# Seven-product multiplication for six column tiles instead of four, with the Fourier groups and the rotation interleaved

## The chip, the cores and the metric

The kernel runs on one core of a Trainium2 chip. The metric is the device time of one execution in microseconds; several runs are taken and the median is given. A core has five engines with their own instruction streams: TensorE (PE, matmuls), VectorE (DVE), ScalarE (ACT), GpSimd (POOL) and SyncE (SP, which here only issues transfers). Each works through its stream in order and waits where an instruction needs something that another engine or a transfer has not finished. Matmuls write to PSUM, which has eight banks of 128 x 512 floats; VectorE and ScalarE read the sums from there.

## The reference

One encoder layer is applied to 768 tokens (a prompt of 512 and a sample of 256) of width 2048:

```
h = rmsnorm(x);  z = h @ w_in            # 2048 x 2560: 1024 Fourier | 1024 q | 256 k | 256 v
of = Re(fft2 over positions and the 128 channels of each of 8 groups), then a 128 x 128 map per group
oa = banded attention on rotated q and k (16 heads, 4 key heads), with a sink per head
x  = x + concat(rmsnorm(of), rmsnorm(oa)) @ w_out
x  = x + relu(rmsnorm(x) @ w_up)**2 @ w_down;  y = rmsnorm(x)
```

The change touches the product z = h @ w_in, the Fourier part and the rotation of q and k. Everything from the attention on is the same code.

## The kernel before

All matmuls are in float32 precision built from three: an operand is split into a rounded high part and the remaining low part (`split`: a copy on ScalarE makes high, a subtraction on VectorE makes low), and high x high, high x low and low x high are summed. w_in has ten column tiles of 256: 0 to 3 Fourier, 4 to 7 queries, 8 keys, 9 values. Work runs through these stages:

**Value columns** (to 44 us): tile 9, as x arrives.

**Seven products** (44 to 161 us): tiles 0 to 3, two pairs of tiles. The weights of a pair are a matrix of 2 x 2 blocks (column tile by half of the 2048 inputs), and so is x (half of the inputs by half of the tokens, 384 each). In place of eight block products the kernel makes seven, Winograd's way, from sums of blocks. They are named a11, s1, s2, s3, a22, s4, a12 after the weight block or sum that they use. Each name takes two pairs g and two halves e of the inner dimension, so 7 x 4 = 28 products, and each product is 24 matmuls of 128 x 128 by 128 x 384 (`product7`, L277): four blocks of the inner dimension, two row halves r of 128 columns, three terms. The loop over n = 0 to 27 makes, for product n, the weight sum three ahead (`sum7`), the high part three ahead (`high7`), the low part two ahead (`low7`), things listed for this n (`high_at`, `low_at`: the sums and splits of x, and near the end `first_split`, which makes the high and low parts of the first quarter of x again for the next stage), the product, the evacuation of the product before it (`out7`) and the load five ahead (`load7`). VectorE, ScalarE and SyncE keep this order as written. PSUM: all eight banks are held, a11, s2, s3 and a22 summing up in the same four; s1, s4 and a12 in others, so that no product waits for a bank.

**Plain pieces** (161 to 365 us): tiles 8, 6, 4, 5, 7 (`cols`), each in four pieces of 48 matmuls (L815). `piece_split(p)` splits the weights of piece p and orders the load of piece p + 2. A list `todo`, filled by `after(piece, fn)`, says after which piece (or half piece) other work is written: for each Fourier group g `fold` (scaling z, sums and differences, and two small matmuls pc of the channel table cc with the map wf), `stage1` and `stage2`, and for each of four pairs of column tiles (keys, then three of the queries) the rotation: `cross` (GpSimd: z times sin), `turned` (VectorE: z times cos, then adds) and `parts` (high and low parts, stored to DRAM). Here TensorE alone keeps the order as written; SyncE, VectorE, ScalarE and GpSimd are put in order by a planner. Group g folds at g + 0.5; the rotation of the pairs begins after piece 10, when the groups are done and their tiles are freed.

The weight tiles `raw` have two buffers, `wh` and `wl` four each, shared by the seven products and the pieces: a load waits until the low part of the weights two loads before is made, and a high part waits until TensorE has finished with the product or piece four before.

## Time and profile before

| | |
|---|---|
| median of 3 runs | 2576.92 us (2576.41 to 2577.49) |
| the profiled execution | 2576.23 us, span 2574.4 us |
| PE busy | 2562.9 us, 13461 matmuls |
| DVE, ACT, POOL busy | 1795.6, 1122.5, 244.2 us |
| seven products, 44.2 to 160.8 us | 116.6 us, PE busy 116.6 |
| plain pieces, 160.8 to 364.6 us | 203.8 us, PE busy 203.8, DVE 113.6 |

A row of a group reads: line, engine, operation, output tile <- input tiles, shapes and count, then busy time in all, mean of one in ns, then the idle time of that engine just before these instructions and what ended it. The mean of a matmul is its latency: matmuls overlap, and the step from one to the next is shorter. A row of the timeline reads: start, duration, engine, line, operation, and in brackets the idle time ahead of it with what ended it. "SPq" is SyncE's queue issuing a transfer.

### The profile page before, as it was taken

The page shows a single profiled execution, that of the slowest core. Times are in us where ns is not written, and L with a number is a line of the kernel's source. Part 1 is how long each engine was busy: PE and PEld are TensorE (multiplying, and loading weights), DVE is VectorE, ACT ScalarE, POOL GpSimd, SP SyncE. Part 2 cuts the span into 40 slices and gives each one's busy share as a digit, 9 for nine tenths or more (in the row PEclk, how much of TensorE's full clock was granted, in tenths as well). Part 3 has the DMA queues.
Part 4 walks back from the last instruction along what each step waited for, and adds up shares of the span by engine and source line. Part 5 has one row for each costly group of instructions (what it writes and reads, how often), then busy time and mean ns, then how long its engine had stood idle before and what let it go on. Part 6 is the DMA issues. An engine that isn't in the chain of part 4 may idle for free.

```text
span 2574.4 us, 34791 instructions
## 1 busy us (share of the span) xinstructions
PE 2562.9 (100%) x13461; PEld 2347.1 (91%) x13461; DVE 1795.6 (70%) x2221; ACT 1122.5 (44%) x1622; POOL 244.2 (9%) x345
## 2 busy tenths in 40 slices
PE   9999999999999999999999999999999999999998
PEld 9999998888899999999999999988888888888887
DVE  7966468786565565556777777667766766777687
ACT  7645337683233333333545544433333333333335
POOL 0102322223201001100000000100000000000000
PEclk9999999999999999999999999999999999999999
DMA  7753567455755455457666666775543662554364
GB/s 290 234 186 126 170 192 214 137 160 191 229 180 176 152 174 174 163 183 240 216 232 230 213 217 211 263 290 175 178 155 118 217 230 83 175 184 159 101 210 152
DMA packets 259383, 487.84 MB, mean 189 GB/s; under 512 B 20554, under 2 KB 146512, under 8 KB 258960
## 3 DMA queue, kind: packets, MB, share of 16 engines
q1 hardware_dynamic: 187680, 321.77, 39.2%
q10 hardware_dynamic: 58512, 112.05, 11.5%
q0 software_dynamic: 13024, 51.79, 6.2%
q8 instruction: 106, 1.74, 0.3%
q14 instruction: 61, 0.50, 0.1%
HBM read 365.99 MB, written 119.54 MB: 189 GB/s over the span
## 4 chain that ended last, share of the span: by engine, by line
PE 98%; DVE 1%; DMA 0%; issue 0%; ACT 0%; SPq 0%; DVEq 0%; POOLq 0%; POOL 0%; ACTq 0%
PE pu L1209 36%; PE pd L1644 35%; PE pm L1062 10%; PE pz L815 6%; PE p L277 5%; PE pv L436 1%; PE o L940 1%; PE s L861 1%; PE t L918 1%; PE pe L644 0%; PE pa L623 0%; PE ptx L137 0%; PE pz L644 0%; DMA xr<-in_x_t 0%; PE pc L580 0%
## 5 line engine op out<-in xcount | busy, mean ns | idle before, releaser
L1209 PE MATMUL pu<-xf,wh 128*128 128x384 f32 x3072 | 780.2, 334 | 0.0
L1209 PEld LDWEIGHTS pu<-xf,wh 128*128 128x128 f32 x3072 | 554.0, 188 | 1.5 <-ACT o L1227 1.3
L1644 PE MATMUL pd<-wl,sh 128*128 128x512 f32 x1332 | 517.7, 389 | 0.0
L1644 PE MATMUL pd<-wh,sh 128*128 128x512 f32 x1332 | 517.7, 389 | 0.0
L1644 PE MATMUL pd<-wh,sl 128*128 128x512 f32 x1332 | 517.5, 389 | 0.0
L1209 PE MATMUL pu<-xf,wl 128*128 128x384 f32 x1536 | 513.1, 334 | 0.0
L1621 ACT ACTIVATE wh<-rd 128x1024 fp32r<-128x1024 f32 x200 | 202.5, 1054 | 522.1 <-PE pd L1644 424.0
L1631 DVE TENSOR_TENSOR wl<-rd,wh 128x1024 fp32r<-128x1024 f32 x200 | 236.2, 1221 | 226.1 <-ACT wh L1621 225.4
L1189 ACT ACTIVATE wh<-ur 128x1024 fp32r<-128x1024 f32 x160 | 170.1, 1063 | 382.7 <-PE pu L1209 204.4
L1644 PEld LDWEIGHTS pd<-wh,sl 128*128 128x128 f32 x1332 | 249.9, 188 | 52.2 <-DVE sl L1632 0.3
L1644 PEld LDWEIGHTS pd<-wh,sh 128*128 128x128 f32 x1332 | 250.0, 188 | 51.7
L1644 PEld LDWEIGHTS pd<-wl,sh 128*128 128x128 f32 x1332 | 250.0, 188 | 51.7
L1209 PEld LDWEIGHTS pu<-xf,wl 128*128 128x128 f32 x1536 | 288.3, 188 | 0.0
L1195 DVE TENSOR_TENSOR wl<-ur,wh 128x1024 fp32r<-128x1024 f32 x160 | 195.5, 1222 | 76.0 <-ACT wh L1189 76.0
L1230 DVE TENSOR_TENSOR o<-pu,o 128x768 f32<-128x768 f32 x160 | 152.9, 956 | 122.5 <-PE pu L1209 115.0
L1614 DVE TENSOR_TENSOR rd<-rd 128x1024 f32<-128x1024 f32 x112 | 131.8, 1218 | 0.0
L1209 PE MATMUL pu<-xs,wh 128*128 128x384 f32 x512 | 129.9, 334 | 0.0
L1189 ACT ACTIVATE wh<-sx 128x1024 fp32r<-128x1024 f32 x64 | 67.8, 1061 | 130.3 <-PE pu L1209 104.9
L277 PE MATMUL p<-xs,wh 128*128 128x384 f32 x448 | 113.7, 334 | 0.0
L1632 DVE TENSOR_TENSOR sl<-sr,sh 128x768 fp32r<-128x768 f32 x111 | 105.6, 951 | 0.0
L1195 DVE TENSOR_TENSOR wl<-sx,wh 128x1024 fp32r<-128x1024 f32 x64 | 78.2, 1223 | 24.1 <-ACT wh L1189 23.9
L1209 PEld LDWEIGHTS pu<-xs,wh 128*128 128x128 f32 x512 | 92.4, 188 | 0.0
(292 smaller groups left out, 3849.1 us busy)
## 6 DMA issues: line engine op xcount, KB each, us to landing
rd<-in_w_down SPq DMA_DIRECT2D x176, 512.0 KB, 5.2
ur<-in_w_up SPq DMA_DIRECT2D x128, 512.0 KB, 3.9
sr<-sd SPq DMA_DIRECT2D x95, 384.0 KB, 5.4
pd<-o ACTq DMA_DIRECT2D x60, 384.0 KB, 2.3
o<-pd POOLq DMA_DIRECT2D x60, 384.0 KB, 6.3
sd<-sm ACTq DMA_DIRECT2D x60, 384.0 KB, 2.9
raw<-in_w_in SPq DMA_DIRECT2D x39, 512.0 KB, 4.1
raw<-in_w_out SPq DMA_DIRECT2D x32, 512.0 KB, 4.6
```

The source lines that it names most:

```text
L277: nc.tensor.matmul(ps7[bank, g, r][:, :HALF], l[:, i, r * P : (r + 1) * P], x[:, o, 4 * e + i, :], start=(opens and e == 0 and i == 0 and ...
L815: nc.tensor.matmul(ps[c][s][:, :HALF], w[:, i, cs], whole[j // 2][s][o][:, 4 * (j % 2) + i, :], start=first and n == 0, stop=stop and n == 2,)
L1062: nc.tensor.matmul(ps, l(k), w[:, k % 2, :], start=(k == 0 and n == 0), stop=(k == 7 and n == 2))
L1189: nc.scalar.activation(wh[:], raw[:], AF.Copy)
L1195: nc.vector.tensor_tensor(out=wl[:], in0=raw[:], in1=f32(wh[:]), op=ALU.subtract)
L1209: nc.tensor.matmul(ps[:, t, :HALF], w[:, i, t * P : (t + 1) * P], xb[:, o, i, :], start=(s == first_of[bank] and i == 0 and n == 0), stop= ...
L1230: nc.vector.tensor_tensor(out=o, in0=src, in1=o, op=ALU.add)
L1614: add = lambda x, y, op: nc.vector.tensor_tensor(out=x[:], in0=x[:], in1=y[:], op=op)
L1621: nc.scalar.activation(wh[:], t[:], AF.Copy)
L1631: nc.vector.tensor_tensor(out=wl[:], in0=t[:], in1=f32(wh[:]), op=ALU.subtract)
L1632: nc.vector.tensor_tensor(out=sl[:], in0=sr[:], in1=f32(sh[:]), op=ALU.subtract)
L1644: nc.tensor.matmul(o, l[:, q, ts], w[:, ns], start=(j == j0 and (q, t) == (0, 0)), stop=(j == j1 and (q, t) == (1, 2)),)
```

## The change

Seven products now serve three pairs of column tiles, (0, 1), (2, 3) and (6, 8), the last one a quarter of the queries and the keys: 7 x 6 = 42 products. The plain pieces keep tiles 4, 5 and 7: 12 pieces. The halves r become the outer loop of a product.

PSUM is shared differently. Six banks ("x") hold the sum that runs through a11, s2, s3 and a22, one for each pair and row half. s1, s4 and a12 have a sum of their own, and these take two banks ("t") by turns. `out7(n, r)` evacuates one row half: r = 0 right after the product, r = 1 an iteration later, ahead of the next product's r = 0. The a11 sums are stored to DRAM and read back for a12 (`back7`), to free their tiles. The x steps in `high_at` and `low_at` are spread over 42 products; `first_split` comes at 35 and 38.

In the pieces, group g folds at g - 0.5, one piece earlier than before, and is loaded half a piece ahead (before: one piece). The first two pairs to be rotated (keys and the first quarter of the queries) are there from the start; the pairs are turned at 0.5, 2.5, 4.5 and 7.5, beside the groups, and the tables cos and sin are loaded before piece 0. [...]

The diff, cut to its core:

```diff
+        cols7 = ((0, 1), (2, 3), (6, 8))
+        NS7 = 2 * len(cols7)
+        NP7 = NS7 * len(names7)
...
         def product7(n):
-            w, g, e = n // 4, n // 2 % 2, n % 2
-            bank = bank7[names7[w]]
-            opens = w == 0 or names7[w] in ("s1", "a12")
+            name, g, e = of7(n)
+            own = name in ("s1", "s4", "a12")
+            opens = own or name == "a11"
             wh, wl = w7.pop(n)
-            if e == 0 and opens:
-                for r in range(2):
-                    ps7[bank, g, r] = pp.tile([P, 512], F32, **(dict(tag="f", bufs=4) if bank == "Y" and 2 * g + r < 4 else dict(tag="ps", bufs=4)), name="p7")
-            x = xs[w % 2]
-            for i in range(4):
-                for r in range(2):
+            x = xs[n // NS7 % 2]
+            for r in range(2):
+                if e == 0 and opens:
+                    ps7[own, g, r] = pp.tile([P, 512], F32, tag="t" if own else "x", bufs=2 if own else 6, name="p7")
+                for i in range(4):
...
-        def out7(n):
-            while put7:
-                put7.pop(0)()
+        def out7(n, r):
             if n < 0 or n % 2 == 0:
                 return
+            s, g, _ = of7(n)
+            ps = ps7[s in ("s1", "s4", "a12"), g, r][:, :HALF]
+            add = lambda out, x: nc.vector.tensor_tensor(out=out[:], in0=ps, in1=x[:], op=ALU.add)
...
+            elif s == "s1":
+                z = c7[1, g, r] = tile7("z11", NS7)
+                nc.scalar.activation(z[:], ps, AF.Copy)
...
+            elif s == "s4":
+                z, put = c7.pop((0, g, r)), (0, 1)
+                add(z, z)
+            else:
+                z, put = c7.pop((2, g, r)), (0, 0)
+                add(z, z)
...
+        def back7(g):
             for r in range(2):
+                z = c7[2, g, r] = tile7("z11", NS7)
+                nc.sync.dma_start(z[:], home7(g, 0, r)[:, :HALF])
...
-        step(low_at, 22, first_block)
-        step(low_at, 20, lambda: first_load(0))
+        step(low_at, 34, first_block)
+        step(low_at, 28, lambda: first_load(0))
         for e in range(2):
-            step(low_at, 24 + 2 * e, lambda e=e: first_split(e))
+            step(low_at, 35 + 3 * e, lambda e=e: first_split(e))
...
                 product7(n)
-                out7(n - 1)
+                out7(n - 1, 1)
+                out7(n, 0)
+                stores7(1 if n % 2 else 0)
                 load7(n + 5)
...
         for g in range(FG):
-            p0 = (0.5, 1.5, 2.5, 3.5, 4.5, 5.5, 6.5, 7.5)[g]
+            p0 = g - 0.5
             if g > 0:
-                after(p0 - 1, lambda g=g: load_group(g))
+                after(p0 - 0.5, lambda g=g: load_group(g))
...
-        for pair, t, ahead in ((0, 10.5, 10), (2, 11.5, None), (3, 15, None), (1, 16.5, 12)):
+        for pair, t in ((0, 0.5), (1, 2.5), (2, 4.5), (3, 7.5)):
...
+        open_rotation()
         with tc.manual_schedule(engines={mybir.EngineType.SP}):
             piece_load(0)
             piece_load(1)
+        load_z(0)
...
-    nc = bacc.Bacc("TRN2", target_bir_lowering=False, num_devices=1)
+    nc = bacc.Bacc("TRN2", target_bir_lowering=False, num_devices=1, dynamic_dma_scratch_size=4096)
```

Three places show how the order of the engines changes. The first is VectorE near the end of the seven products, around the second `first_split` (L73). In these rows wl is a low part of weights, xf the low part of x, and z<-p the add that evacuates a sum p. Before:

```order
L262 TENSOR_TENSOR wl<-raw,wh 128x1024
L70 TENSOR_TENSOR wl<-raw,wh 128x1024
L73 SCALAR_TENSOR_TENSOR xf_1608<-d_1679,gall,xf_1607 128x384 x4
L294 TENSOR_TENSOR z_892<-p_1681,z_892 128x384
L294 TENSOR_TENSOR z_894<-p_1682,z_894 128x384
L70 TENSOR_TENSOR wl<-raw,wh 128x1024 x2
```

And now:

```order
L300 TENSOR_TENSOR z_1994<-p_2119,z_1994 128x384
L272 TENSOR_TENSOR wl<-wr,wh 128x1024
L73 SCALAR_TENSOR_TENSOR xf_2038<-d_2086,gall,xf_2037 128x384 x4
L300 TENSOR_TENSOR z_1996<-p_2132,z_1996 128x384
L272 TENSOR_TENSOR wl<-raw,wh 128x1024
L70 TENSOR_TENSOR wl<-raw,wh 128x1024
```

The add of a product's first half (p_2119) stands before the split, that of its second half (p_2132) behind it; both belong to product 37 and its banks are the ones that product 38 opens again.

The second is SyncE at the transition from the products to the pieces (L237 and L331 are `load7` and `back7`, L79 the pieces' weights, cc and wf the operands of the first pc, tab a table of positions). Before:

```order
L227 DMA raw<-in_w_in 128x1024
L79 DMA raw<-in_w_in 128x1024 x6
L564 DMA cc<-in_c_chan 128x256
L559 DMA wf<-in_w_fourier 128x128
L561 DMA zf<-zf_70 128x768
L570 DMA tab<-in_c_pos 128x512
L559 DMA wf<-in_w_fourier 128x128
L570 DMA tab<-in_c_pos 128x512
L561 DMA zf<-zf_71 128x768
```

And now:

```order
L237 DMA raw<-in_w_in 128x1024
L79 DMA raw<-in_w_in 128x1024 x6
L603 DMA cc<-in_c_chan 128x256
L598 DMA wf<-in_w_fourier 128x128
L600 DMA zf<-zf_70 128x768
L609 DMA tab<-in_c_pos 128x512
L711 DMA cosr<-in_c_cos 128x768
L711 DMA sinr<-in_c_sin 128x768
L730 DMA zs<-zs_78 128x2x768
L609 DMA tab<-in_c_pos 128x512
L598 DMA wf<-in_w_fourier 128x128 x2
L600 DMA zf<-zf_71 128x768
```

cc and wf stand behind six piece loads as before; behind them now come cos, sin and the first pair to be rotated (zs), ahead of the second group's zf.

The third is VectorE within a Fourier group's turn in the pieces: from the scaling of one group's zf to the low part sl of its sums, on which its stage 1 waits. Before:

```order
L576 TENSOR_TENSOR zf<-zf,rb 128x768
L617 TENSOR_TENSOR ft<-pa,ft 128x256
L70 TENSOR_TENSOR al<-ft,ah 128x256
L70 TENSOR_TENSOR al<-pa,ah 128x256
L70 TENSOR_TENSOR cw<-pc,cw 128x256
L70 TENSOR_TENSOR al<-pa,ah 1x128
L70 TENSOR_TENSOR wl<-raw,wh 128x1024
L70 TENSOR_TENSOR sl<-fs,sh 128x768
```

And now:

```order
L70 TENSOR_TENSOR cw<-pc,cw 128x256
L746 TENSOR_TENSOR zs<-zs,cosr 128x2x256
L759 TENSOR_TENSOR zs<-zs,zh 128x2x256
L748 TENSOR_TENSOR zs<-zs,zy 128x256 x2
L70 TENSOR_TENSOR wl<-raw,wh 128x1024
L746 TENSOR_TENSOR zs<-zs,cosr 128x2x256
L70 TENSOR_TENSOR sl<-fs,sh 128x768
L70 TENSOR_TENSOR al<-pa,ah 128x256
```

The rows that write zs are the rotation's: L746 needs the pair and cos, L748 GpSimd's product zy, L759 ScalarE's high part zh.

## The prediction

> **What bounds the kernel now.** I read the page first: busy shares (section 1), then the shares of the chain that ended last (section 4).

> ```profile
> PE 2562.9 (100%) x13461; PEld 2347.1 (91%) x13461; DVE 1795.6 (70%) x2221; ACT 1122.5 (44%) x1622; POOL 244.2 (9%) x345
> ...
> PE 98%; DVE 1%; DMA 0%; issue 0%; ACT 0%; SPq 0%; DVEq 0%; POOLq 0%; POOL 0%; ACTq 0%
> PE pu L1209 36%; PE pd L1644 35%; PE pm L1062 10%; PE pz L815 6%; PE p L277 5%; PE pv L436 1%; PE o L940 1%; PE s L861 1%; PE t L918 1%; PE pe L644 0%; PE pa L623 0%; PE ptx L137 0%; PE pz L644 0%; DMA xr<-in_x_t 0%; PE pc L580 0%
> ```

> TensorE is busy for 2562.9 of 2574.4 us and is the chain. The lines that the change touches are p L277 (the seven products, 5%) and pz L815 (the plain column tiles, 6%). Next the waits of PE, all of them:

> ```profile
> PE pv L436 <- ACT xs L417: 1.1, 1, 1.1
> PE pw L457 <- DVE ssx L132: 1.0, 1, 1.0
> PE pv L436 <- ACT xs L69: 0.6, 1, 0.6
> PE pm L1064 <- DVE ofl L1046: 0.2, 1, 0.2
> ```

> Four waits, 2.9 us, none in the stages that change. So PE has nothing to gain there but matmuls, and every wait that the change brings is a loss. Third, the stretches from the stage windows (busy PE, PEld, DVE, ACT, POOL, then granted clock, DMA share, GB/s) and from the chain of waits for the steps:

> ```profile
> 44.20:160.80 116.60, 116.60 (x675) 116.51 (x674) 94.22 (x86) 71.17 (x99) 11.55 (x18) 1.00 0.64 213
> 160.80:364.60 203.80, 203.80 (x1277) 203.60 (x1277) 113.63 (x220) 77.54 (x174) 49.41 (x40) 1.00 0.50 161
> ...
> 44.36 91.53 PE p L277 x528
> 160.96 12.48 PE pz L815 x72
> 289.75 74.86 PE pz L815 x431
> ```

> PE is full in both stretches at clock 1.00. A matmul of 384 columns costs a step of 91.53/528 = 0.1734 us (74.86/431 = 0.1737 for pz), so a product (24 matmuls) takes 4.16 us and a plain piece (48) 8.33 us.

> **The change, term 1: matmuls.** Seven products serve six column tiles in place of four: 14 products more, 14 x 24 = 336 matmuls. Plain pieces go from 20 to 12: 8 x 48 = 384 fewer. Net 48 fewer x 0.1735 = **-8.3 us**. This is the whole gain; it can't be larger, because the rest of PE's work is the same.

> **Term 2: two banks by turns.** s1, s4 and a12 share two PSUM banks, so that a product that opens a bank waits for the add or copy of the sum before it. With the row half r outermost, a bank is closed half a product (2.08 us) before it is opened again. What the add costs, and what can stand ahead of it in DVE's queue:

> ```profile
> L262 DVE TENSOR_TENSOR wl<-wr,wh 128x1024 fp32r<-128x1024 f32 x11 | 13.4, 1219 | 9.5 <-ACT wh L254 9.5
> L314 DVE TENSOR_TENSOR xs<-xr,xs 128x1536 fp32r<-128x1536 f32 x10 | 17.5, 1752 | 1.9 <-ACT xs L311 1.6
> L294 DVE TENSOR_TENSOR z<-p,z 128x384 f32<-128x384 f32 x10 | 5.1, 548 | 0.0
> L297 ACT ACTIVATE z<-p 128x384 f32<-128x384 f32 x16 | 6.9, 477 | 0.4 <-PE p L277 0.4
> ```

> For s1 the copy is ScalarE's, behind one 128x1024 copy at most: 1.06 + 0.48 = 1.5 us of 2.08, no wait. For s4 the add after product 31 stands behind a sum, a low part and the low part of the other operand: the first half's add ends about 2.7 us into product 31, and the second half's 1.22 + 1.22 + 1.75 + 0.55 = 4.7 us later, 0.4 us less for overlapping ends: 7.0 after product 31's start, 2.9 to 3.0 after product 32's. That bank is needed at 2.08: **about 0.9**. For a12 two adds stand behind first_split, four scaled copies on ScalarE and four low parts on VectorE. Of that the trace has the very rows, before the change:

> ```profile
> 144.19 1.06 ACT L254 ACTIVATE wh<-raw 128x1024 fp32r<-128x1024 f32 x1 [3.10 <-PE p L277]
> 145.15 2.12 ACT L72 ACTIVATE xf<-d,gall 128x384 fp32r<-128x384 f32 x4
> 145.78 2.21 DVE L73 SCALAR_TENSOR_TENSOR xf<-d,gall,xf 128x384 fp32r<-128x384 f32 x4 [3.44 <-ACT xf L72]
> 147.91 1.02 DVE L294 TENSOR_TENSOR z<-p,z 128x384 f32<-128x384 f32 x2
> ```

> ScalarE's split starts when PE ends a product (144.19); the low parts end at 147.99, 3.8 us later, and an add (1.02 for two) 0.5 after that: 4.3, with 0.2 from the product's last issue to ScalarE's start 4.5. Before, this held up nobody, since no bank was waited for. In the change product 38's second half needs its bank 2.08 into the product: **a wait of 2.4**. Product 36 opens its bank a whole product, 4.16, after the first split began: 4.5 - 4.16 = 0.3. Sum **+3.6**, bounds +1 (only the 2.4, and half of it hidden) to +5.

> **Term 3: the first fold.** pc of group 0, which needs cc and wf from DRAM, moves from half a piece after piece 0 (160.96 + 12.48: after 72 matmuls) to the middle of piece 0 (24 matmuls, 4.17 us). SyncE's order keeps both loads behind six piece loads, and the sixth waits for its buffer until the low part of piece 3 is made:

> ```profile
> 165.81 1.23 DVE L70 TENSOR_TENSOR wl<-raw,wh 128x1024 fp32r<-128x1024 f32 x1 [2.95 <-ACT wh L69]
> ...
> 150.12 17.27 SPq L79 DMA_DIRECT2D raw<-in_w_in  x5
> 167.44 0.43 SPq L564 DMA_DIRECT2D cc<-in_c_chan  x1
> 167.92 0.42 SPq L559 DMA_DIRECT2D wf<-in_w_fourier  x1
> ...
> wf<-in_w_fourier SPq DMA_DIRECT2D x3, 64.0 KB, 4.5
> cc<-in_c_chan SPq DMA_DIRECT2D x1, 128.0 KB, 4.0
> ```

> Here the low part ends at 167.04 and cc is issued at 167.44, 0.4 later; wf 0.5 after cc, landing 4.0 to 4.5 later: 0.4 + 0.5 + 4.3 = 5.2 after that low part. In the change piece 3's split can't start before product 41 ends, since it takes over that product's buffer: 0.2 + 1.06 + 1.23 puts the low part at 2.4 into piece 0 (overlapping ends), wf at 7.4 or so, and pc is due at 4.2: **+3.0**, bounds 2 (a fast landing) to 4. Before, pc was due at 12.5 and these loads were hidden.

> **Term 4: Fourier groups and rotation side by side.** Before, VectorE turned the four pairs after piece 10; now pairs 0, 1 and 2 are turned within pieces 0 to 6, beside eight groups. The groups of VectorE and GpSimd in the second stretch:

> ```profile
> L70 DVE TENSOR_TENSOR wl<-raw,wh 128x1024 fp32r<-128x1024 f32 x21 | 26.2, 1249 | 29.3 <-ACT wh L69 29.2
> L709 DVE TENSOR_TENSOR zs<-zs,zy 128x256 f32<-128x256 f32 x24 | 11.3, 507 | 0.0
> L707 DVE TENSOR_TENSOR zs<-zs,cosr 128x512 f32<-128x512 f32 x12 | 10.4, 864 | 7.4 <-POOL zy L700 7.4
> L726 DVE SCALAR_TENSOR_TENSOR zs<-zs,zh 128x512 fp32r<-128x512 f32 x9 | 7.1, 805 | 2.0 <-ACT zh L725 2.0
> L723 DVE TENSOR_TENSOR zs<-zs,zh 128x512 fp32r<-128x512 f32 x3 | 2.6, 861 | 0.0
> L700 POOL TENSOR_TENSOR zy<-zs,sinr 128x256 f32<-128x256 f32 x24 | 22.4, 958 | 33.4 <-ACT zs L828 22.8 <-DVE zs L709 9.9 <-DVE sinr L680 0.6
> ```

> A pair costs (11.3 + 10.4 + 7.1 + 2.6)/4 = 7.9 us of durations, a split 1.25. The window's busy 113.6 less 4 x 7.9, 21 splits and some 4 us of single operations is 52; ends of neighbours overlap, so I take 6.5 to 7 for a group, 7.3 for a pair, 1.15 for a split. The piece's time with its group on PE is 8.33 + (203.8 - 20 x 8.33)/8 = 13.0 at most, 12.8 with the last matmuls taken off. Two pieces then ask 2 x 6.8 + 7.3 + 2 x 1.15 = 23.2 of 25.6 us, and a pair brings (7.4 + 2.0)/4 = 2.3 us of waits for GpSimd and ScalarE, in which everything behind stands too: 25.5 of 25.6. VectorE has no slack there, where before it was busy for 113.6 of 203.8, 56%. The start is late as well: cos, sin and the first pair (1.5 MB) are loaded among the group's own loads at some 210 GB/s, and behind them stand the sums and the low part sl that the first stage-1 matmuls need. By hand sl(0) comes about 1 us late, and the second stages of groups 0 to 2 follow late by similar amounts. Bounds: 0 (the waits fall where VectorE would be idle) to 3 x 2.5 + 1 = 8.5 (nothing of it is hidden). No row shows the mix; I take the middle, **+4.4**.

> [...] GpSimd's product and VectorE's, in time order:

> ```profile
> 299.48 1.26 DVE L707 TENSOR_TENSOR zs<-zs,cosr 128x512 f32<-128x512 f32 x1 [0.63 <-POOL zy L700]
> 303.09 0.68 DVE L707 TENSOR_TENSOR zs<-zs,cosr 128x512 f32<-128x512 f32 x1
> ...
> 299.45 1.88 POOL L700 TENSOR_TENSOR zy<-zs,sinr 128x256 f32<-128x256 f32 x2
> 303.33 2.71 POOL L700 TENSOR_TENSOR zy<-zs,sinr 128x256 f32<-128x256 f32 x2 [2.00 <-DVE zs L709]
> ```

> Beside GpSimd the product took 1.26, alone 0.68. [...]

> **The rest at nothing.** The a11 sums that go to DRAM and back are read some twenty products after they were stored. The row norms keep two products (8.3 us) between their steps in place of three. [...] Bounds 0 to +2 together.

> **Sum.** -8.3 + 3.6 + 3.0 + 4.4 = +2.7 us. The profiled execution took 2576.2 us (span 2574.4, and 1.8 around it, which nothing here changes), so 2578.9; the median of the runs, 2576.9, lies 0.7 above it, and would give 2579.6. I say **2579**. The terms' bounds give -8.3 + 1 + 2 + 0 = -5.3 to -8.3 + 5 + 4 + 8.5 + 2 = +11.2, that is 2571 to 2587.

> **Rivals.**
> *Cover holds.* DVE absorbs the rotation (its mean over the new stretch is only (113.6 - 8 x 1.25)/(203.8 - 66.6) = 76%), the loads land faster, and at most the 2.4 us wait is left: -8.3 to -5.9, about **2569**, faster. For it: no wait at all in these stages before. Against it: the 144.19 rows and the order of SyncE's queue, which are not averages.
> *VectorE's queue becomes the bound of pieces 0 to 6.* From the point where two pieces ask over 25.6 us, each pair costs PE its waits: term 4 at 8.5 or above, -8.3 + 3.6 + 3.0 + 8.5 = +6.8, **2583**, and 2586 if GpSimd's products hold up the Fourier sums as well (18 x 0.2). Slower. For it: the 25.5 above. Against it: much of VectorE's time falls between deadlines.
> *The saving does not arrive for another reason*: the two banks cost more than reckoned, because an add waits behind a low part whose high part waits for PE: the five openings of a used bank by s4 and a12 at 2.4 us each give 12 us in place of 3.6, -8.3 + 12 + 3.0 + 4.4 = +11.1, **2587**. Against it: only the two splits have ScalarE in the way.

> **How the numbers follow.** A difference under 0.2% (5.2 us) can't be told from none. The likeliest, 2579 with its own range of 2572 to 2582, is no change: chance 0.43. Cover holds: 0.24, faster. VectorE's queue 0.28 and the banks 0.05: slower, 0.33. The range, 2570 to 2587, takes in the bounds and most of each rival.

> **What would show it.** Of the after profile: PE should have 48 rows fewer at these lines, and L286 and L852 should step at 0.1735 as before. PE's waits should name DVE z (an add) at product 38, about 2.4 us, and at 32, about 1; a wait of pc for wf or cc, about 3, in piece 0; and waits of pa or pe for DVE sl or al within pieces 1 to 4. If PE's waits in the whole stretch sum to under 3 us the forecast is wrong to the fast side; if those of pa and pe alone pass 8 us, VectorE's queue is the bound. A difference after 365 us, in stages that do not change, would be none of these.

## The result: slower by 0.7%

The changed kernel takes 2594.31 us (median of 4 runs, 2591.74 to 2596.34) against 2576.85 before: ratio 1.0068, 95% interval 1.0056 to 1.0080, so 17.5 us slower. The forecast was 2579, range 2570 to 2587. The profiled execution took 2596.3 us, 2 us above the median, span 2594.6; the sums below are of this one. Its page, busy shares and chain:

```profile
PE 2566.5 (99%) x13413; PEld 2347.5 (90%) x13413; DVE 1821.6 (70%) x2247; ACT 1126.1 (43%) x1622; POOL 249.9 (10%) x345
...
PE 87%; DVE 3%; POOL 1%; issue 1%; ACT 0%; DMA 0%; SPq 0%; ACTq 0%; DVEq 0%; POOLq 0%
```

The 48 matmuls are gone (13461 to 13413), but PE is busy for 3.6 us longer, and it fell from 98% to 87% of the chain. The stage windows of after (length, then busy PE, PEld, DVE, ACT, POOL, granted clock, DMA share, GB/s):

```profile
45.00:228.00 183.00, 177.52 (x1011) 176.18 (x1010) 128.33 (x121) 87.24 (x115) 11.55 (x18) 0.99 0.64 212
228.00:385.40 157.40, 146.56 (x894) 143.87 (x893) 103.69 (x210) 65.08 (x159) 54.70 (x40) 0.96 0.53 173
385.40:2594.00 2208.60, 2201.04 (x11210) 1986.59 (x11208) 1554.42 (x1861) 938.65 (x1285) 183.50 (x283) 1.00 0.56 187
```

and the last of them before the change:

```profile
364.60:2574.00 2209.40, 2201.12 (x11209) 1986.15 (x11208) 1552.63 (x1861) 938.61 (x1285) 183.10 (x283) 1.00 0.57 188
```

From the attention on nothing changed (2208.6 us against 2209.4), so the last line of the diff, `dynamic_dma_scratch_size=4096`, cost nothing there that shows. All is lost in two stages: the products take 183.0 us where 1008 steps of 0.1735 are 174.9, and the pieces 157.4 where 203.8 less 384 steps (66.7) would be 137.1. What PE waits for in after, from 44 to 400 us:

```profile
PE pc L619 <- ACT of L685: 4.2, 4, 1.7
PE pz L683 <- DVE al L70: 3.7, 4, 2.0
PE p L286 <- DVE z L300: 3.2, 3, 2.2
PE pc L619 <- DMA wf<-in_w_fourier: 2.6, 1, 2.6
PE p L286 <- ACT z L307: 2.3, 1, 2.3
PE pz L683 <- ACT ah L69: 0.2, 1, 0.2
```

These are 16.2 us. The rest is in how matmuls step after a wait, as PE's timeline shows:

```profile
209.31 0.34 PE L286 MATMUL p<-xs,wl 128*128 128x384 f32 x1
211.81 1.01 PE L286 MATMUL p<-xs,wh 128*128 128x384 f32 x2 [2.15 <-DVE z L300]
212.61 0.52 PE L286 MATMUL p<-xs,wl 128*128 128x384 f32 x1
212.93 0.84 PE L286 MATMUL p<-xs,wh 128*128 128x384 f32 x2
```

After the wait for the add a matmul takes 0.52 in place of 0.34, and the next starts 0.32 later (212.61 to 212.93) in place of 0.17, until about 215.2. The windows show the granted clock (third number from the end) in that time, and in the slices ahead:

```profile
78.63:82.05 3.42, 1.94 (x12) 1.61 (x10) 2.56 (x3) 0.70 (x1) 0.00 (x0) 1.00 0.95 383
...
208.34:211.75 3.41, 1.31 (x8) 0.99 (x6) 2.67 (x6) 2.22 (x5) 0.00 (x0) 1.00 0.15 58
211.75:215.17 3.42, 3.36 (x10) 3.37 (x11) 1.13 (x2) 0.00 (x0) 0.00 (x0) 0.50 0.49 146
```

The trace of after has the granted clock at 0.50 in four stretches between 45 and 385 us: 211.75 to 215.17, 235.65 to 239.06, 276.61 to 283.43 and 297.09 to 300.50. Each is 3.41 us long or twice that, and their starts lie 23.9, 41.0 and 20.5 us apart, whole multiples of 3.41. Divided into slices of that length from these starts, the trace gives how long PE stood still in each: 2.10 us in the slice from 208.34, and the one behind it is at 0.50, while the equally long wait at product 8 (80.6 to 82.8) fell into two slices, 1.48 us into the first and 0.79 into the second, and the clock stayed at 1.00. The slices ahead of the other three stretches, a slice behind which the clock stayed at 1.00 (259.54) and one within the stretch from 276.61:

```profile
232.23:235.65 3.42, 0.87 (x7) 0.77 (x7) 0.00 (x0) 0.02 (x1) 0.00 (x0) 1.00 0.93 291
...
259.54:262.95 3.41, 1.86 (x15) 1.73 (x14) 3.41 (x8) 1.44 (x6) 0.41 (x1) 1.00 0.46 159
...
273.19:276.61 3.42, 1.45 (x11) 1.19 (x10) 3.27 (x11) 1.34 (x7) 0.11 (x1) 1.00 0.67 218
276.61:280.02 3.41, 2.93 (x14) 2.74 (x13) 2.15 (x6) 1.15 (x3) 1.96 (x3) 0.50 0.63 176
...
293.67:297.09 3.42, 1.69 (x15) 1.55 (x14) 3.35 (x8) 1.14 (x2) 0.00 (x0) 1.00 0.48 151
```

PE stood still for 2.55, 1.97 and 1.73 us in the three and for 1.55 in the one that kept the clock; 0.48 within the stretch was followed by 0.50 again.

The balance, summed over the starts of all PE rows from 44 to 385 us (the usual step of a line and its tiles is the median; a step of over 0.4 us is a wait, counted at its length less the usual step):

| part | us |
|---|---|
| matmuls saved | -8.3 |
| bank turns: s1 2.4, s4 1.1, a12 0.3 and 2.3, with 0.3 in the step behind it | +6.4 |
| wait for wf | +2.8 |
| waits in the Fourier groups | +10.1 |
| slow matmuls, an estimate: half of the 16.5 us that PE is busy at granted clock 0.50 (1.7 in the products, 6.6 in the pieces) | +8.3 |
| start of the products (varies from run to run, 41.6 to 45.0 us) | +0.8 |
| sum; the spans differ by 20.2 | +20.1 |

Counted from start to start, the three rows of waits come to 19.3 us; the waits view has 16.2 for the same 14 waits, 0.2 less for each in the mean.

### The profile page after: what moved, and what is told of

The parts are those of the page before. It is cut to its first block, busy times and chain, and to the rows that moved or that the text cites. A ratio compares the mean times of both kernels' runs of the same rounds, so it can differ in the third digit from the quotient of the medians.

```text
span 2594.6 us, 34763 instructions
## 1 busy us (share of the span) xinstructions
PE 2566.5 (99%) x13413; PEld 2347.5 (90%) x13413; DVE 1821.6 (70%) x2247; ACT 1126.1 (43%) x1622; POOL 249.9 (10%) x345
## 4 chain that ended last, share of the span: by engine, by line
PE 87%; DVE 3%; POOL 1%; issue 1%; ACT 0%; DMA 0%; SPq 0%; ACTq 0%; DVEq 0%; POOLq 0%
PE pu L1240 36%; PE pd L1675 35%; PE pm L1093 10%; PE pz L852 2%; PE o L971 1%; PE t L949 1%; PE s L892 1%; PE p L286 1%; POOL zy L739 0%; PE ptx L137 0%; DVE zs L748 0%; DVE zs L746 0%; DMA zs<-zs 0%; DVE al L70 0%; DVE fs L624 0%
## 5 line engine op out<-in xcount | busy, mean ns | idle before, releaser
L286 PE MATMUL p<-xs,wh 128*128 128x384 f32 x672 | 172.1, 337 | 5.5 <-DVE z L300 3.2
L286 PEld LDWEIGHTS p<-xs,wh 128*128 128x128 f32 x672 | 122.0, 189 | 6.8 <-DVE z L300 3.7
L286 PE MATMUL p<-xs,wl 128*128 128x384 f32 x336 | 112.8, 336 | 0.0
```

The source lines that it names most:

```text
L286: nc.tensor.matmul(ps7[own, g, r][:, :HALF], l[:, i, r * P : (r + 1) * P], x[:, o, 4 * e + i, :], start=(opens and e == 0 and i == 0 and q ...
```

## The experiments

The median of the kernel before lay between 2576.1 and 2576.9 in all comparisons, so that medians can be set beside each other.

**The bank turns.** Edit: the second row half is evacuated at the head of the iteration.

```diff
             for n in range(NP7):
+                out7(n - 1, 1)
                 for fn in high_at.get(n, ()):
...
                 product7(n)
-                out7(n - 1, 1)
                 out7(n, 0)
```

> The changed kernel with one edit: the evacuation of a product's second row half is written first in the next iteration, ahead of the sums and low parts, where the change has it last. In the changed kernel's profile PE waits 6.4 us in the seven products for adds and a copy of the two banks, and 1.3 us more go into matmuls that step at 320 ns instead of 173 after the last of these waits. Theory 1 (the order of the queue is the whole cause): these waits vanish and no new ones come, 2594 - 7.7 = about 2586.5. Rival (no slack on VectorE there): weights' low parts come late instead and PE waits for wl; 2590 or more.

Measured: 2587.91 us, ratio to before 1.0040 (1.0025 to 1.0055). Of the waits at the turns this is left:

```profile
PE p L286 <- DVE z L300: 0.2, 1, 0.2
```

The order in the queue was the cause. In after itself both faces of it can be read, VectorE and ScalarE at s1, then at a12:

```profile
80.03 1.22 DVE L256 TENSOR_TENSOR ws<-wr,raw 128x1024 f32<-128x1024 f32 x1 [0.86 <-DMA raw<-in_w_in]
81.35 1.06 ACT L264 ACTIVATE wh<-ws 128x1024 fp32r<-128x1024 f32 x1 [3.41 <-DVE ws L256]
82.31 0.47 ACT L307 ACTIVATE z<-p 128x384 f32<-128x384 f32 x1
...
208.45 2.12 ACT L72 ACTIVATE xf<-d,gall 128x384 fp32r<-128x384 f32 x4
209.08 2.21 DVE L73 SCALAR_TENSOR_TENSOR xf<-d,gall,xf 128x384 fp32r<-128x384 f32 x4 [1.86 <-ACT xf L72]
211.20 0.55 DVE L300 TENSOR_TENSOR z<-p,z 128x384 f32<-128x384 f32 x1
```

The copy that frees a bank (82.31) is 0.47 us long, but stands behind a high part that waited 3.41 us for a sum, which waited for a load. The length of this wait hangs on the loads: in the five other kernels below that leave the products as they are it was 0.6 to 2.1 us, 0.6 where VectorE waited 0.3 us for the loads of these sums; here it waited 1.7.

**The start of the first group.** Edit: cc and wf of group 0 in tiles of their own, loaded at product 30.

```diff
+                if n == 30:
+                    nc.sync.dma_start(cc[:], a["c_chan"])
+                    nc.sync.dma_start(wf0[:], a["w_fourier"][0])
```

> The changed kernel with one edit: the channel table cc and the map wf of group 0 get tiles of their own and are loaded during product 30. Theory: pc in piece 0 no longer waits (2.8 us in the changed kernel's profile) and the 1.7 us that the matmuls behind it lose at half speed do not come: 2594 - 4.5 = 2589.8. Rival: the wait only moves, because zf, cos, sin and the first pair are still behind six piece loads; the first stage-1 matmuls then wait for sl instead: 2592 or more.

Measured: 2594.21 us. The rival was right. The wait for wf is gone and these stand in its place:

```profile
PE pa L655 <- ACT sh L69: 1.7, 1, 1.7
PE pa L656 <- DVE sl L70: 0.7, 1, 0.7
```

The next link of the chain, zf to sums to sh and sl, was nearly as late as wf. From 44 to 400 us PE waits 3.1 us less than in after (13.1 against 16.2), but its granted clock is at 0.50 for 23.9 us in place of 17.1: with PE busy for 21.8 of them that costs, by the same estimate of a half, 10.9 us in place of 8.3, and takes the gain. The opposite edit puts the groups back by a piece:

```diff
-            p0 = g - 0.5
+            p0 = g + 0.5
...
-        after(9, fourier_norm)
-        after(9, open_attention)
+        after(10, fourier_norm)
+        after(10, open_attention)
```

> The changed kernel with the Fourier groups back at g + 0.5, one piece later as before the change, and what follows them (norm, opening of the attention's tiles, loads of k and q) one piece later too; the rotation stays where the change put it. All theories: the 2.8 us wait for wf and the 1.7 us of slow matmuls behind it vanish. Theory of the late start: the groups' waits vanish with it, 2594 - 4.5 - 10 = about 2580. Theory of VectorE's queue: the waits move to later pieces and half or more stay, 2585 to 2590.

Measured: 2598.82 us, slower still. The waits of the groups did not vanish with the late start, as the theory of VectorE's queue has it (10.8 us stay), but its price, 2585 to 2590, was too low; and the attention now began late:

```profile
PE pz L683 <- DVE al L70: 6.4, 4, 3.4
PE pm L1093 <- ACT ofh L1076: 4.1, 1, 4.1
```

**The rotation beside the groups.** Three kernels; the first leaves out the arithmetic of the rotation for pairs 0 to 2, the second only GpSimd's product for them, the third computes all and has that product on VectorE:

```diff
-                nc.gpsimd.tensor_tensor(out=y[:, b], in0=zt[pair][:, 1 - b, ts], in1=kt["sinr"][:, ts], op=ALU.mult)
+                nc.vector.tensor_tensor(out=y[:, b], in0=zt[pair][:, 1 - b, ts], in1=kt["sinr"][:, ts], op=ALU.mult)
```

> The changed kernel, leaving out all arithmetic of the rotation for pairs 0, 1 and 2 (GpSimd's products, VectorE's products, adds and low parts, ScalarE's high parts); the loads and stores stay. In the changed kernel PE waits 10.1 us between 245 and 365 us for the Fourier groups, and loses some 5 us more in matmuls at half speed. Theory 1 (rotation in VectorE's queue holds the Fourier operations up): the waits fall under 2 us and the slow matmuls with them, leaving the wait for wf: 2594 - 13 = about 2581. Rival (the groups start one piece too early and their own loads and chain are late): at least half of the waits stay, 2587 or more.

Measured: 2583.23 us (2579.14 to 2587.20), 11.1 us less. The first theory was right. In the pieces of the profiled execution (2579.23 us) PE waits for this and no more:

```profile
PE pc L619 <- DMA wf<-in_w_fourier: 2.6, 1, 2.6
PE pz L683 <- DVE al L70: 0.4, 1, 0.4
```

> The changed kernel, leaving out only GpSimd's product z times sin for pairs 0, 1 and 2; VectorE does the same operations in nearly the same order, its adds reading z in place of that product. Theory 1a (VectorE's own work is too much): of the 10.1 us of waits at least 7 stay, 2591 or more. Theory 1b (what holds VectorE's queue is waiting for GpSimd, and running slower beside it): the waits fall under 3 us, about 2582 to 2584.

Measured: 2586.28 us. Between the two theories, nearer to GpSimd: 8.0 us less in all, with 4.0 us of such waits left of 8.1 (and, by the profiled execution, 1.7 us less of the wait at product 8, which has nothing to do with the edit):

```profile
PE pc L619 <- ACT of L685: 3.2, 3, 1.7
...
PE pz L683 <- DVE al L70: 0.8, 1, 0.8
```

> The changed kernel with one edit: the rotation's product z times sin on VectorE instead of GpSimd, in all pairs. VectorE gets 24 products of some 0.4 us more, and its operations no longer wait for GpSimd's or run beside them. If waiting for GpSimd and running beside it is what counts (leaving the product out took 8 us off): about 2586 to 2588. If VectorE's load counts as much: 2594 or more.

Measured: 2587.24 us. The same product on the busier engine is 7.1 us faster:

```profile
PE pz L683 <- DVE al L70: 1.8, 2, 1.3
PE pc L619 <- ACT of L685: 0.5, 1, 0.5
```

So it is the rotation, and within it not VectorE's load, but GpSimd's product. It reaches VectorE's queue in two ways, which these runs do not separate: VectorE waits for it, and what VectorE does beside it takes longer. Both show at the first pair of after, in GpSimd's products and VectorE's:

```profile
242.23 6.56 POOL zy L739 x4
...
246.97 1.21 DVE L746 TENSOR_TENSOR zs<-zs,cosr 128x512 f32<-128x512 f32 x1 [1.31 <-POOL zy L739]
248.82 0.69 DVE L746 TENSOR_TENSOR zs<-zs,cosr 128x512 f32<-128x512 f32 x1 [0.63 <-POOL zy L739]
```

GpSimd's four products, 0.96 us each in the kernel before, take 6.56 together here. VectorE waits 1.31 and 0.63 us for them, and its own product takes 1.21 us beside them, 0.69 when they are done. From VectorE the delay goes on to ScalarE, whose copy of pe (L685) is what PE waits for in 4.2 of the 8.1 us; at 295.80 it stands behind the rotation's high part zh, which waits for VectorE:

```profile
295.26 0.63 ACT L761 ACTIVATE zh<-zs 128x512 fp32r<-128x512 f32 x1 [3.06 <-DVE zs L748]
295.80 0.60 ACT L685 COPY of<-pe 128x512 f32<-128x512 f32 x1
```

**The order, asked for or written.** Edit of the first: evacuation first, cc and wf early, and thirds of a pair one piece apart:

```diff
-        for pair, t in ((0, 0.5), (1, 2.5), (2, 4.5), (3, 7.5)):
+        for pair, ts in ((0, (0.5, 1.5, 2.5)), (1, (3.5, 4.5, 5.5)), (2, (6.5, 7.5, 8.5)), (3, (9, 9.5, 10))):
```

> Three edits on the changed kernel: evacuation first (measured alone: 2587.9), cc and wf of group 0 early, and the rotation asked for in thirds, one piece apart (pair 0 at 0.5, 1.5, 2.5, pair 1 at 3.5, 4.5, 5.5, pair 2 at 6.5, 7.5, 8.5, pair 3 at 9, 9.5, 10), where the change asks for a pair's thirds within half a piece. The planner still orders VectorE, and its rows show rotation ahead of Fourier work as soon as a pair is there. If the asked piece decides: the 10.1 us of Fourier waits fall under 3, about 2573. If VectorE's order decides: the two first edits alone act, 2594 - 6.4 - 4.5 = 2583, and most of the 10.1 us stays.

Measured: 2589.19 us, 1.3 more than the evacuation alone and neither forecast: 7.4 us of Fourier waits stay, so the asked piece does not decide, and 3.8 us of new wait for ofh come at the attention's start.

> Evacuation first, early cc and wf, and the same spread thirds, but with the planner's order on all engines but TensorE. Differs from the kernel with three edits (2589.2) only in that pair 3 is rotated a piece earlier and pairs 0 to 2 half a piece to a piece earlier. Theory (the 4.1 us before attention came from the late pair 3, whose buffers the attention's first tiles take over): that wait goes, 2589 - 4 - 1.7 = about 2583; the Fourier waits, about 7 us, stay.

Measured: 2585.36 us; that wait is gone, as the buffers' theory says, and 9.0 us of Fourier waits stay.

> As the kernel with three edits, but VectorE keeps the written order within the pieces: per piece the end of the second stage, the first stages and the fold of a group, then one third of a rotation, then the split of a weight piece; SyncE, ScalarE and GpSimd stay with the planner. The work on VectorE is the same to within the order. Theory (order of the queue, not the sum of work: 23.2 of 25.6 us for two pieces fits): Fourier waits under 3 us, 2594 - 6.4 - 4.5 - 12 = about 2571, faster than the kernel before by some 5 us. Rival (VectorE's and GpSimd's work is simply too much side by side): 5 us of waits or more stay, 2577 or more.

Measured: 2601.67 us. My theory of the order alone fell:

```profile
PE pz L859 <- ACT zs L868: 10.7, 1, 10.7
PE pm L1100 <- ACT ofh L1083: 7.0, 1, 7.0
```

Low parts (al) no longer held up PE, but a late rotation holds the tiles that pieces and attention take over, and short copies on ScalarE came late (5.9 us of PE's waits). With all three engines in written order:

> Evacuation first and early cc and wf as before, and within the pieces VectorE, ScalarE and GpSimd all keep the written order; the rotation's thirds are spread (pair 0 at 0.5, 1, 1.5, pair 1 at 2.5, 3.5, 4.5, pair 2 at 5.5, 6.5, 7.5, pair 3 at 8, 8.5, 9), and the scaling and storing of a group's output comes half a piece later. With VectorE's order alone (2601.7) the waits of PE for al had gone, but PE waited 10.7 us for banks that ScalarE could not empty and 7.0 for the attention's first tile, both because rotation tiles were freed late, and 5.9 us in pc for ScalarE's copy of pe. Theory: what counts is that no short operation that PE waits for stands behind a wait in the queue of any of the three engines; the waits after the pieces' start fall under 3 us: 2594 - 6.4 - 12 = about 2575. Rival: three engines in written order wait for one another in turn, 5 us or more stay, 2578 or more.

Measured: 2612.91 us, the slowest of all; the rival was right.

```profile
PE pc L623 <- ACT of L689: 11.5, 5, 4.1
PE pm L1105 <- ACT ofh L1088: 8.6, 1, 8.6
```

**The slow matmuls.** Built-in waits in the kernel before; `stalls = {4: 0, 8: 1, 12: 2, 16: 4, 20: 5, 24: 7}` gives the small operations for each product:

```diff
+            if n in stalls:
...
+                nc.vector.tensor_copy(wl[:, 0, :], ps7[bank7[s], g, 1][:, :256])
+                for _ in range(stalls[n]):
+                    nc.vector.tensor_tensor(out=wl[:, 0, :], in0=x[:, 0, :], in1=f32(wl[:, 0, :]), op=ALU.max)
             nc.vector.tensor_tensor(out=wl[:], in0=x[:], in1=f32(wh[:]), op=ALU.subtract)
...
             for n in range(NP7):
+                if n in stalls:
+                    low7(n)
```

> The kernel before, with six waits built in among the seven products, every fourth product from 4 to 24: the low part of the product's weights is made only after VectorE has read the sum of the product before and done 0, 1, 2, 4, 5 or 7 small operations. Expected waits of PE 1.6 to 4 us. Theory of a window: a wait over some 2 us is followed by matmuls at 320 ns for up to 3.4 us in some cases and not in others, shorter ones never, longer ones nearly always; each such phase costs 1.3 to 1.7 us. Rival: only waits of 3.4 us or more have that effect; then the phases in the changed kernel have another cause.

Measured: waits of 4.6, 1.9, 2.3, 3.3, 3.7 and 4.6 us (the first is longer than built), and behind each of the six a phase in which matmuls step at 320 ns, costing 1.2 to 2.5 us. This is one execution of the kernel. The shortest wait, with the slice in which it lies and the one behind it:

```profile
85.26 0.45 PE L284 MATMUL p<-xs,wl 128*128 128x384 f32 x1 [1.88 <-DVE wl L269]
...
82.64:86.05 3.41, 1.53 (x9) 1.21 (x8) 2.91 (x4) 0.00 (x0) 0.00 (x0) 1.00 0.00 0
86.05:89.46 3.41, 3.41 (x13) 3.41 (x12) 3.41 (x4) 1.82 (x3) 0.00 (x0) 0.50 0.59 177
```

The rival falls: waits well under 3.4 us were enough. The six stretches at 0.50 begin 20.5 or 23.9 us apart, again whole multiples of 3.41, and are 3.41 us long, one of them 6.83. The length of a wait alone does not tell which is followed by such a phase: in after the 2.3 us wait at s1 was not, the 2.2 us wait at a12 was. By slices, PE stood still for 1.88 us ahead of the 0.50 here and for 1.73 to 2.55 us ahead of the four stretches of after, and for up to 1.55 us where the clock stayed at 1.00 there; but within the stretch from 276.61 it was 0.48 us, and the half clock went on. These are the cases measured; no rule follows from them.

**The causes taken away together.** Evacuation first; cc, wf and zf of group 0 loaded during the products; z times sin on VectorE. The new part of it:

```diff
+        zf0 = hp.tile([P, T], F32, tag="zf0", name="zf0")
...
+                if n == 39:
+                    nc.sync.dma_start(zf0[:], zf_d[0][:])
```

> Three causes taken away together from the changed kernel: the second row half is evacuated first; cc, wf and zf of group 0 have tiles of their own and are loaded during the products (the identity's tile holds wf meanwhile, the first group's tile later holds ssf), so that the whole chain to the first stage 1 starts early; and z times sin is made on VectorE. If the three causes (evacuation order 7.7 us with its slow phase, start of the first group 4.5 with its slow phase, GpSimd beside and ahead of VectorE some 7 of 10, plus its slow phases) add up: 2594.3 - 7.7 - 4.5 - 9 = about 2573, faster than the kernel before by 3 us. If VectorE's load takes the place of GpSimd's waits once the start is early: 2578 to 2582.

Measured: 2577.31 us, ratio to before 1.0004 (0.9995 to 1.0012): 17 us less than the change, and no difference from before.

> The same without the third edit: z times sin stays on GpSimd. Evacuation order and the start of the first group alone: 2594.3 - 7.7 - 4.5 = about 2582; the waits of PE for al and for ScalarE's copy of pe stay, 5 us or more. Rival (the groups were late only because the first one was): they fall under 3 us and the time is that of the kernel with the product on VectorE, within 1 us.

Measured: 2585.62 us: without the third edit 8.3 us more, and over 9 us of waits in the groups. The groups were not late only because the first one was. Between the evacuation alone (2587.91) and this, the early start alone is worth 2.3.

> All three edits and the rotation in thirds (pair 0 at 0.5, 1, 1.5, pair 1 at 2.5, 3.5, 4.5, pair 2 at 5.5, 6.5, 7.5, pair 3 at 8, 8.5, 9). If the bursts of three thirds at once still hold up Fourier operations with the product on VectorE: 2 us less than the kernel with the three edits. If the planner hoists the rotation anyway, as its rows show: the same within 1 us.

Measured: 2577.29 us: bursts are not a fourth cause. What is left in the kernel with three edits shows where VectorE (first two rows) and GpSimd meet:

```profile
275.28 0.74 DVE L750 TENSOR_TENSOR zy<-zs,sinr 128x256 f32<-128x256 f32 x2
277.21 3.35 DVE L750 TENSOR_TENSOR zy<-zs,sinr 128x256 f32<-128x256 f32 x2
...
276.52 1.76 POOL L703 TENSOR_TENSOR sq<-of 128x768 f32<-128x768 f32 x1 [10.91 <-DVE of L695]
278.36 1.91 POOL L704 TENSOR_TENSOR ssf<-ssf,sq 128x768 f32<-128x768 f32 x1
```

The same two products take 0.74 us alone and 3.35 while GpSimd squares and sums. The longest wait of PE in this kernel comes from GpSimd's squares in another way:

```profile
250.03 0.94 ACT L705 ACTIVATE of<-of,gall 128x768 f32<-128x768 f32 x1 [4.88 <-POOL ssf L700]
251.31 0.42 DVE L70 TENSOR_TENSOR al<-ft,ah 128x256 fp32r<-128x256 f32 x1 [2.31 <-ACT ah L69]
257.98 0.58 PE L690 MATMUL pz<-tabh,al 128*128 128x256 f32 x1 [1.98 <-DVE al L70]
```

ScalarE scales a group's output in place, and so only when GpSimd has squared it; in the pieces it waits 15.5 us for that. The high part ah stands behind the scaling, VectorE waits 2.31 us for ah, and has hardly a gap from there to the low part for which PE waits. So the last edit takes the squares off GpSimd too, and with them both the work beside VectorE and ScalarE's waits:

```diff
-                nc.gpsimd.tensor_tensor(out=sq[:], in0=of[:], in1=of[:], op=ALU.mult)
-                nc.gpsimd.tensor_tensor(out=ssf[:], in0=ssf[:], in1=sq[:], op=ALU.add)
+                nc.scalar.activation(sq[:], of[:], AF.Square)
+                nc.vector.tensor_tensor(out=ssf[:], in0=ssf[:], in1=sq[:], op=ALU.add)
```

> The kernel with three causes taken away (2577.3), and GpSimd without work in the pieces: the squares of a group's output are made on ScalarE and summed up on VectorE. In that kernel two VectorE products that take 0.74 us take 3.35 while GpSimd squares and sums (276.5 to 280.3 us), and PE still waits some 5 us in the pieces with 4 us of slow matmuls. If GpSimd beside VectorE is the last cause: the waits fall under 2 us, 2577 - 5 to 7 = 2570 to 2572, faster than the kernel before. If VectorE's load (8 sums of 0.9 us more) takes its place: 2576 to 2580.

Measured: 2571.51 us, ratio 0.9982 (0.9973 to 0.9990), as forecast for GpSimd as the last cause. Which of its two ways weighs how much is not shown: the edit takes both away.

> The same with the rotation in thirds. With GpSimd idle, bursts of the rotation are what is left ahead of Fourier operations: if they matter, 1 to 2 us less than the kernel without thirds; if not, the same within 1 us.

Measured: 2571.21 us, ratio 0.9978 (0.9968 to 0.9987): 5.5 us faster than before, the best of all, and no different from the one ahead of it. The window of its pieces:

```profile
218.00:364.00 146.00, 143.59 (x924) 142.48 (x923) 109.16 (x253) 72.29 (x169) 2.28 (x1) 1.00 0.58 190
```

and the largest of PE's waits:

```profile
PE pc L626 <- ACT of L692: 2.4, 4, 1.1
```

VectorE is busier here than in the changed kernel (109.2 of 146.0 us against 103.7 of 157.4), GpSimd has one operation left (2.28 us), and the clock is at 1.00 from 45 us to the attention. Of the 8.3 us of matmuls some 5 arrive.

## Why the prediction was wrong

**Term 1** (-8.3) was right: 48 matmuls fewer, at the same step wherever PE didn't wait.

**Term 2** (+3.6, measured 6.4). a12 was right (2.4 and 0.3; measured 2.3 and 0.3), s4 nearly (0.9; 1.1). The step that failed is "behind one 128x1024 copy at most: 1.06 + 0.48 = 1.5 us of 2.08, no wait" for s1: it counted how long the copy ahead takes, and not what that copy waits for. Most of product 8's wait of 2.4 us came from loads, through two engines.

**Term 3** (+3.0, measured 2.8) was right in place, cause and size, though its own steps give 2.4 + 5.2 - 4.2 = 3.4. As a price for what the wait costs it misled: taking that wait away alone gained nothing.

**Term 4** (+4.4, bounds 0 to 8.5; measured 10.1) was too small, and the mechanism is the second rival's only in part. VectorE's queue does hold PE up, but in 4.2 of the 8.1 us by way of ScalarE's copy of pe, and at pc and pz where pa and pe were expected. Nor was the sum of work the matter: 25.5 of 25.6 us was taken as the point from which it decides, yet with more work on VectorE and next to none on GpSimd only 2.4 us of the 8.1 are left. Two steps failed. One is that only the rotation's own rows, the lengthened 1.26 among them, were reckoned as work beside GpSimd: GpSimd squares the groups' outputs as well, and Fourier operations beside it took longer too (al<-ft in the kernel before 0.90 us at 211.18, beside ssf, and 0.42 at 198.37 with GpSimd idle). The other is the sum of 25.5 itself, which has waits for the rotation, (7.4 + 2.0)/4 for each pair, and none for the groups, where VectorE waits for ah behind ScalarE's scaling and GpSimd's squares. Both stood in the profile before, in a row that the prediction does not show. Here it is for the kernel before, the changed one and the best one:

```profile
L70 DVE TENSOR_TENSOR al<-ft,ah 128x256 fp32r<-128x256 f32 x8 | 6.3, 782 | 15.3 <-ACT ah L69 15.3
...
L70 DVE TENSOR_TENSOR al<-ft,ah 128x256 fp32r<-128x256 f32 x8 | 5.4, 680 | 8.3 <-ACT ah L69 8.3
...
L70 DVE TENSOR_TENSOR al<-ft,ah 128x256 fp32r<-128x256 f32 x8 | 3.3, 418 | 0.3
```

15.3 us of waits for eight groups are 1.9 for each, 3.8 for the two that share two pieces with a pair. In the kernel before VectorE had room for them, and PE waited for none of them; in the change the sum leaves 25.6 - 25.5 = 0.1 us.

The second rival's 18 x 0.2 us, for Fourier sums held up by GpSimd's products, is shown by no run. What the runs show in its place: al<-ft takes 0.62 to 0.90 us beside GpSimd in after and 0.41 to 0.42 without, two of VectorE's products take 3.35 us beside sq and ssf and 0.74 without (with three edits), and with GpSimd's product on VectorE the changed kernel takes 7.1 us less.

**What no term had** are the 8.3 us of slow matmuls. The step that failed here is the price of a matmul, 0.1735 us for L286 and L852 as before, taken to hold throughout. PE's clock was read as 1.00 in the kernel before, and that it would hold was taken as given; here it is 0.50 for 17.1 us behind waits, and the step there nearly doubles (173 to 320 ns). The longer waits alone, 6.4 + 2.8 + 10.1 - 8.3 = +11.0, would have given 2587, the upper end of the range; the slow matmuls took it out of there.

The first rival (cover holds, 2569) and the third (banks at every turn, 2587) are out: the turns cost 6.4 us, at four places.

What stays open: what brings on the half clock (it came behind 0.48 us of standing still within a stretch, and not behind 1.55), how much of GpSimd's cost is waiting for it and how much is working beside it, and whether the 0.8 us before the products is more than scatter.

## What to carry to other kernels

Where TensorE is the bound and never waits, price a wait not by its length alone: here the slow matmuls behind 19 us of waits added 8, and the wait for wf taken away alone left the time as it was (2594.31 and 2594.21 us). When a bank, a tile or a short copy becomes something that the bound engine waits for, look at what stands ahead of it in its queue, and at what each of those waits for in turn; writing the evacuation first in the iteration was worth 6.4 us. Work handed to GpSimd was not free here, beside a busy VectorE: moving 24 products and the groups' squares off it, on to engines that had less room, gained some 14 us (8.3 and 5.8).
